# One low-part split in four by an accumulating DMA instead of VectorE, in the feed-forward weights of a hybrid decoder block

## The chip, the cores and the metric

The kernel runs on one core of a Trainium2 chip. Time is device time in microseconds (us) for one execution of the whole program. The engines are named as in the profile: PE is TensorE (matrix multiply; PEld its weight loads), DVE is VectorE, ACT is ScalarE, POOL is GpSimd, SP is SyncE, which here only issues DMAs.

## The reference

One layer of a decoder block, 256 tokens, model width 2048, all float32: a normalised input goes through an input projection into two token mixers (a Mamba-2 scan and a causal pooling), their outputs through an output projection; then a feed-forward part of width 5632, a residual add and a final norm. What matters here is the feed-forward part:

```python
def swiglu(h, w_gate, w_up, w_down):
    return (jax.nn.silu(h @ w_gate) * (h @ w_up)) @ w_down
...
h = h + swiglu(rms_norm(h, ffn_norm_w[i]), w_gate[i], w_up[i], w_down[i])
return rms_norm(h, final_norm_w)
```

The three weights are 2048 x 5632, 2048 x 5632 and 5632 x 2048 numbers; they are read from HBM once.

## The kernel before

The feature dimension lies on partitions, tokens on the free dimension. Every weight is multiplied as two float32r parts, `w = hi + lo`, and so is every activation; three of the four products are formed (`mm_part`, L191): for each k-tile of 128 rows and each block of 128 columns one matmul of `hi` with the activation's high and low parts side by side (512 columns, L206) and one of `lo` with the high part (256 columns, L214).

`WeightStream` (L37) makes those parts. Weights come in pieces, lists that are written out in the order of use (L127 to L168): for the feed-forward part 22 groups of 256 columns, each with two pieces of 8 k-tiles from `w_gate` and two from `w_up`, then 8 groups of `w_down` with five pieces of 8 k-tiles and one of 4. SP loads each piece into a raw buffer (three buffers, L67 and L74), and each piece is split in chunks of 4 k-tiles (128 x 1024 elements): ACT copies the raw chunk into `hi`, which rounds it (L89), and DVE subtracts, `lo = raw - hi` (L90). So there are 8 chunks in a gate and up pair, 4 each, and 11 in a down group: 264 in the feed-forward part.

`hi` and `lo` have three buffers each (`AHEAD`, L41). `next` (L95) hands chunk n to the matmuls and first emits the splits up to chunk n + 2; the split of a chunk can start when the matmuls of the chunk three before it have released its buffers. The engines work through their queues in order; a scheduler places the instructions, and the splits are marked to go early:

```python
with self.tc.high_priority():
    nc.scalar.copy(out=hi[:, :nk, :], in_=raw)
    nc.vector.tensor_tensor(
        out=lo[:, :nk, :], in0=raw, in1=hi[:, :nk, :].bitcast(F32), op=ALU.subtract)
```

After a gate or up group (`for f in range(NFG)`, L628) ACT and DVE take the sums out of PSUM: for gate a copy (L635), an add (L636), a multiplication (L637) and the SiLU on ACT (L638); for up a copy (L642), three DVE operations (L643 to L645), and the split of the hidden values into `hid` (L650, L651). Down groups end in `evac_add` (L599) and a few operations for the norm. POOL does almost nothing: four loads of the decays `E` (L488), the load of the residual `h` (L581), and one operation at the end.

Of the kernel before, what the change touches and what calls it, by code (L numbers as in the profile page):

```python
# [14 lines left out]
T = 256  # L15
# [11 lines left out]

# columns of the packed per-channel vectors
V_ATTN, V_CONVW, V_CONVB, V_DSKIP, V_SSDN, V_PSC, V_FFN, V_FIN, V_ALL = (
    0, 16, 112, 136, 152, 168, 184, 200, 216)  # L30

# 256-column groups of the input projection in the order they are consumed:
# B (0, 1), C (2, 3), u (4..11), then per SSD group two of x and two of z
G_U, G_XZ = 4, 12


class WeightStream:  # L37
    """Weights in order of use: loaded ahead, then split exactly into two
    float32r parts (w = hi + lo) in chunks of up to four k-tiles."""

    AHEAD = 3  # L41

    def __init__(self, tc, pool, pieces):
        self.tc, self.nc, self.pool = tc, tc.nc, pool
        # a piece is a list of (source, k-tiles) that are loaded into one buffer
        self.pieces = pieces
        self.chunks = []
        for p, srcs in enumerate(pieces):
            base = 0
            for i, (_, nk) in enumerate(srcs):  # L50
                k0 = 0
                while k0 < nk:
                    n = 2 if p == 0 and i == 0 else 4
                    self.chunks.append((p, base + k0, n))
                    k0 += n
                base += nk
        self.after_load = {}
        self.raw = {}
        self.split = {}
        self.loaded = 0  # L60
        self.done = 0
        self.pos = 0
# [17 lines left out]
    def split_to(self, n):  # L80
        nc = self.nc
        while self.done < min(n, len(self.chunks)):
            p, k0, nk = self.chunks[self.done]
            self.load_to(p + 3)
            raw = self.raw[p][:, k0:k0 + nk, :]
            hi = self.pool.tile([P, 4, 256], F32R, tag="hi", name=f"hi{self.done}", bufs=self.AHEAD)
            lo = self.pool.tile([P, 4, 256], F32R, tag="lo", name=f"lo{self.done}", bufs=self.AHEAD)
            with self.tc.high_priority():
                nc.scalar.copy(out=hi[:, :nk, :], in_=raw)  # L89
                nc.vector.tensor_tensor(  # L90
                    out=lo[:, :nk, :], in0=raw, in1=hi[:, :nk, :].bitcast(F32), op=ALU.subtract)
            self.split[self.done] = (hi, lo, nk)
            self.done += 1
# [9 lines left out]
def kernel(  # L103
# [22 lines left out]

# [1 line left out]
    pieces = []  # L128
# [29 lines left out]
    for g in range(2, 8):  # L158
        add_out(g, 1)
        add_out(g, 0)  # L160
    for f in range(NFG):
        for w in (w_gate, w_up):
            pieces.append([(w[f, :, 0:8, :], 8)])
            pieces.append([(w[f, :, 8:16, :], 8)])
    for g in range(8):
        for k in range(0, KF, 8):
            nk = min(8, KF - k)
            pieces.append([(w_down[g, :, k:k + nk, :], nk)])  # L168
    stream = WeightStream(tc, wpool, pieces)

# [1 line left out]
    vec_sb = const.tile([P, V_ALL], F32, name="vec_sb")  # L172
# [18 lines left out]
    def mm_part(ps, rhs, first, last, wide=True):  # L191
        """ps[b][:, 0:256] += w_hi x_hi + w_lo x_hi for the two 128-column blocks b, over
        the k-tiles whose [hi | lo] are in rhs; w_hi x_lo goes to ps[b][:, 256:512]
        when wide, and to ps[b][:, 0:256] too when not."""
        if not isinstance(ps, list):
            ps = [ps[:, 0, :], ps[:, 1, :]]
        k = 0
        n = len(rhs)
        while k < n:
            hi, lo, nk = stream.next()  # L200
            for b in range(2):
                cs = slice(b * P, (b + 1) * P)
                for j in range(nk):
                    st = first and k + j == 0
                    if wide:
                        nc.tensor.matmul(  # L206
                            ps[b], hi[:, j, cs], rhs[k + j],
                            start=st, stop=False, skip_group_check=True)
                    else:
                        for o in (0, T):  # L210
                            nc.tensor.matmul(  # L211
                                ps[b][:, 0:T], hi[:, j, cs], rhs[k + j][:, o:o + T],
                                start=(st and o == 0), stop=False, skip_group_check=True)
                    nc.tensor.matmul(  # L214
                        ps[b][:, 0:T], lo[:, j, cs], rhs[k + j][:, 0:T],
                        start=False, stop=(last and k + j == n - 1), skip_group_check=True)
            k += nk
# [6 lines left out]
    def rstd_stats(sqs, n, name):  # L224
        """1/sqrt(EPS + sum over partitions and over the list of sqs / n), with tokens on
        partitions, as the diagonals of two [128, 128] matrices."""
        pss = [pms.tile([P, 512], F32, tag="ms", name=f"ps{c}_{name}") for c in range(2)]
# [19 lines left out]
    def rstd_spread(stats, c=0):  # L247
        """The result of rstd_stats, [128, 256], the same on every partition, in PSUM."""
        pss, dg = stats
        ps = pss[c][:, T:512]  # L250
        nc.tensor.matmul(ps, ones, dg.rearrange("p c t -> p (c t)"), start=True, stop=True,
                         skip_group_check=True)
        return ps

    # ================= phase 1: norm, input projection, mixers =================
    xhl = big.tile([P, KD, 512], F32R, tag="big", name="xhl")
# [51 lines left out]
    def evac_in(ps, dst):  # L308
        """dst = ps * rstd for the two blocks of an input-projection group."""
        nc.vector.tensor_tensor(out=dst, in0=ps[:, :, 0:T], in1=bc_mid(r1, 2), op=ALU.mult)  # L310

    def conv_silu(dst, src, ct, pool):
        """dst = silu(causal depthwise conv of src) for channel tile ct."""
        o = pool.tile([P, T], F32, tag="cv", name="cv", bufs=2)
        w = [col(V_CONVW, 4 * ct + k) for k in range(4)]
        nc.scalar.activation(o, src, AF.Identity, scale=w[3], bias=col(V_CONVB, ct))
        for s in (1, 2, 3):
            tap = nc.vector.scalar_tensor_tensor(
                out=o[:, s:T], in0=src[:, 0:T - s], scalar=w[3 - s], in1=o[:, s:T],
                op0=ALU.mult, op1=ALU.add)  # L320
        return tap, nc.scalar.activation(dst, o, AF.Silu)
# [17 lines left out]

# [1 line left out]
    dtT = p1.tile([P, 2, NHEAD], F32, name="dtT")  # L341
    nacT = p1.tile([P, 2, NHEAD], F32, name="nacT")
    acum_d = dram.tile([NHEAD, T], F32, name="acum_d")
    with tc.tile_pool(name="pd", bufs=1) as pd:
# [20 lines left out]
        nc.vector.tensor_scalar(v, v, hvec_sb[:, 0:1], None, op0=ALU.add)  # L365
        # softplus(v) = max(v, 0) + log1p(e), e = exp(-|v|); log1p(e) = 2 atanh(e / (2 + e))
        nc.vector.scalar_tensor_tensor(out=e, in0=v, scalar=-1.0, in1=v, op0=ALU.mult, op1=ALU.max)
# [31 lines left out]
    def cb_group(g):  # L399
        """C B^T of a group: s in the first tile against all l, then s and l in the second."""  # L400
        cbp = pms.tile([P, 512], F32, tag="ms", name="cbp")
# [5 lines left out]
    def x_group(g, c):  # L407
        """A 256-column group of x, normalised; the conv comes later."""
        ps = mm_group(xk, f"x{g}_{c}", wide=False)
        xin = p1.tile([P, 2, T], F32, tag="xin", name="xin", bufs=2)  # L410
        evac_in(ps, xin)
        return xin

# [1 line left out]
    with tc.tile_pool(name="pp", bufs=1) as pp:  # L415
# [60 lines left out]

# [1 line left out]
    with tc.tile_pool(name="psd", bufs=1) as pssd:  # L478
# [5 lines left out]
        for g in range(NGRP):  # L484
            # log-decays, causal mask, exp
            E = pssd.tile([P, HPG, 384], F32, tag="E", name="E", bufs=1)
# [90 lines left out]

    # ================= phase 2: output projection, FFN, final norm =================
    p2 = ctx.enter_context(tc.tile_pool(name="p2", bufs=1))
# [10 lines left out]
    def add_sq(k):  # L590
        """ssq += squares of h1's k-tiles k, k + 1."""
        t2 = squares(k)
# [6 lines left out]
    def evac_add(ps, k):  # L599
        """h1[k, k + 1] += a + b."""  # L600
        tb = p2.tile([P, 2, T], F32, tag="tb2", name="tb2", bufs=2)
# [50 lines left out]

    # the last SiLU is done: bring in the square root's table before the tail needs it
    nc.scalar.activation(warm, hid[2][:, KF - 2 * KD - 1, T - 1:T].bitcast(F32), AF.Sqrt, scale=0.0)
# [81 lines left out]
```

## Time and profile before

| what | us |
|---|---|
| three executions | 1308.55, 1309.37, 1324.73 |
| their median | 1309.37 |
| span of the profiled execution | 1322.4 |
| PE busy in it | 1309.8 (99%) |
| DVE, ACT, POOL busy | 836.0 (63%), 665.6 (50%), 9.0 (1%) |

The profile is of one execution, whose span runs from its first instruction to its last. Only the execution of 1324.73 us is long enough to hold it, so that is taken as the profiled execution's own time: 2.3 us lie around the span. Busy times add up an engine's instructions; matmuls overlap, so a matmul's duration (0.40 us for 512 columns) is longer than the step from one to the next. A row names an instruction by its line, engine, operation, and output<-inputs. In square brackets stands how long the engine was idle before it and what ended that.

### The profile page before, as it was taken

Reading aid. Unit: us, or ns where it says so; the run is one execution under the profiler, and the core shown is the slowest. Engines: PE = TensorE matmul, PEld = TensorE weight load, DVE = VectorE, ACT = ScalarE, POOL = GpSimd, SP = SyncE. Lnnn points to the kernel's source line nnn. Section 1 sums busy time; section 2 is a strip of 40 time slices with the busy share of each in tenths; the row PEclk is TensorE's granted clock in tenths of the full one; section 3 lists DMA queues with packets and bytes.
Section 4 is the critical chain, followed back from the end, with each engine's and each line's share of the span. In section 5 each row is a group of like instructions: output and inputs, shape, how many; then the busy total and the mean of one; then the engine's idle time right before and its main releaser. Section 6 shows DMA issues by size and latency. Waiting matters only on the chain.

```text
span 1322.4 us, 20341 instructions
## 1 busy us (share of the span) xinstructions
PE 1309.8 (99%) x8490; PEld 1184.9 (90%) x8490; DVE 836.0 (63%) x1017; ACT 665.6 (50%) x823; POOL 9.0 (1%) x23
## 2 busy tenths in 40 slices
PE   9999999999999999999999999999999999999996
PEld 8999999999998888888888888888888888888896
DVE  6977877878776556565656556565656554555453
ACT  7644447677674444454444444444444444444442
POOL 0000000000000000000000000000000000000000
PEclk9999999999999999999999999999999999999998
DMA  8445556555546555555555555555555555555552
GB/s 301 157 164 188 191 178 212 186 193 186 196 160 250 181 180 187 189 186 187 177 188 186 191 192 188 180 182 186 187 191 191 186 181 181 199 176 184 198 176 80
DMA packets 36844, 247.08 MB, mean 187 GB/s; under 512 B 4080, under 2 KB 4368, under 8 KB 8976
## 3 DMA queue, kind: packets, MB, share of 16 engines
q1 hardware_dynamic: 35376, 239.10, 53.0%
q0 software_dynamic: 1232, 6.29, 1.3%
q8 instruction: 66, 1.08, 0.3%
q10 hardware_dynamic: 144, 0.39, 0.1%
q14 instruction: 26, 0.21, 0.0%
HBM read 243.64 MB, written 2.13 MB: 186 GB/s over the span
## 4 chain that ended last, share of the span: by engine, by line
PE 98%; DMA 1%; DVE 0%; SPq 0%; ACT 0%; issue 0%; DVEq 0%
PE up L206 13%; PE g L206 13%; PE d L206 11%; PE o L206 9%; PE d L214 6%; PE g L214 6%; PE up L214 6%; PE x L211 5%; PE u L211 5%; PE z L211 5%; PE o L214 5%; PE u L214 2%; PE x L214 2%; PE z L214 2%; PE bc L211 2%; PE d L211 2%
## 5 line engine op out<-in xcount | busy, mean ns | idle before, releaser
L90 DVE TENSOR_TENSOR lo<-raw,hi 128x1024 fp32r<-128x1024 f32 (+1 forms) x449 | 548.2, 1221 | 434.1 <-ACT hi L89 432.8
L89 ACT CAST hi<-raw 128x1024 fp32r<-128x1024 f32 (+1 forms) x449 | 469.9, 1047 | 597.2 <-PE d L206 122.1
L206 PE MATMUL g<-h1hl,hi 128*128 128x512 f32 x704 | 249.9, 399 | 0.0
L206 PE MATMUL up<-h1hl,hi 128*128 128x512 f32 x704 | 249.6, 399 | 0.0
L206 PE MATMUL d<-hid,hi 128*128 128x512 f32 x616 | 217.7, 399 | 0.0
L214 PE MATMUL d<-hid,lo 128*128 128x256 f32 x704 | 197.9, 281 | 0.0
L214 PE MATMUL g<-h1hl,lo 128*128 128x256 f32 x704 | 197.7, 281 | 0.0
L214 PE MATMUL up<-h1hl,lo 128*128 128x256 f32 x704 | 197.6, 281 | 0.0
L206 PEld LDWEIGHTS g<-h1hl,hi 128*128 128x128 f32 x704 | 132.3, 188 | 33.1
L206 PEld LDWEIGHTS up<-h1hl,hi 128*128 128x128 f32 x704 | 132.3, 188 | 32.9
L206 PEld LDWEIGHTS d<-hid,hi 128*128 128x128 f32 x616 | 115.7, 188 | 28.8
L214 PEld LDWEIGHTS g<-h1hl,lo 128*128 128x128 f32 x704 | 133.0, 189 | 0.0
L214 PEld LDWEIGHTS d<-hid,lo 128*128 128x128 f32 x704 | 133.0, 189 | 0.0
L214 PEld LDWEIGHTS up<-h1hl,lo 128*128 128x128 f32 x704 | 133.0, 189 | 0.0
L211 PE MATMUL z<-xhl,hi 128*128 128x256 f32 x512 | 93.3, 285 | 0.0
L211 PE MATMUL x<-xhl,hi 128*128 128x256 f32 x512 | 93.0, 284 | 0.0
L211 PE MATMUL u<-xhl,hi 128*128 128x256 f32 x512 | 93.0, 283 | 0.0
L206 PE MATMUL o<-yssd,hi 128*128 128x512 f32 x256 | 91.0, 399 | 0.0
L206 PE MATMUL o<-ypool,hi 128*128 128x512 f32 x256 | 90.6, 398 | 0.0
L211 PEld LDWEIGHTS x<-xhl,hi 128*128 128x128 f32 x512 | 79.8, 192 | 0.5 <-issue 0.5
L211 PEld LDWEIGHTS z<-xhl,hi 128*128 128x128 f32 x512 | 79.9, 192 | 0.2
L211 PEld LDWEIGHTS u<-xhl,hi 128*128 128x128 f32 x512 | 80.0, 192 | 0.0
(189 smaller groups left out, 1603.9 us busy)
## 6 DMA issues: line engine op xcount, KB each, us to landing
raw<-in_w_in_dram SPq DMA_DIRECT2D x52, 1024.0 KB, 5.0
raw<-in_w_gate_dram SPq DMA_DIRECT2D x44, 1024.0 KB, 5.0
raw<-in_w_up_dram SPq DMA_DIRECT2D x44, 1024.0 KB, 5.1
raw<-in_w_down_dram SPq DMA_DIRECT2D x40, 1024.0 KB, 4.8
raw<-in_w_out_dram SPq DMA_DIRECT2D x32, 1024.0 KB, 4.8
raw<-in_pool_w_dram SPq DMA_DIRECT2D x4, 1024.0 KB, 4.9
E<-acum_d POOLq DMA_DIRECT2D x4, 1024.0 KB, 5.9
raw<-in_w_down_dram SPq DMA_DIRECT2D x8, 512.0 KB, 3.3
```

The lines of the kernel that those rows point to most:

```text
L89: nc.scalar.copy(out=hi[:, :nk, :], in_=raw)
L90: nc.vector.tensor_tensor(out=lo[:, :nk, :], in0=raw, in1=hi[:, :nk, :].bitcast(F32), op=ALU.subtract)
L206: nc.tensor.matmul(ps[b], hi[:, j, cs], rhs[k + j], start=st, stop=False, skip_group_check=True)
L211: nc.tensor.matmul(ps[b][:, 0:T], hi[:, j, cs], rhs[k + j][:, o:o + T], start=(st and o == 0), stop=False, skip_group_check=True)
L214: nc.tensor.matmul(ps[b][:, 0:T], lo[:, j, cs], rhs[k + j][:, 0:T], start=False, stop=(last and k + j == n - 1), skip_group_check=True)
```

## The change

In chunks of four k-tiles that belong to a feed-forward piece and whose number is divisible by 4, `lo` is no longer made by DVE. ACT first writes `-hi` into `lo`; then POOL issues a DMA that reads the same weights from HBM a second time and adds them onto `lo`, so that `lo = -hi + w`. The raw piece is loaded as before, since `hi` is still made from it. The rest of the difference between the two files is comments that went, so that later lines move by 9.

```diff
+        self.dma_from = len(pieces)
...
             with self.tc.high_priority():
                 nc.scalar.copy(out=hi[:, :nk, :], in_=raw)
-                nc.vector.tensor_tensor(
-                    out=lo[:, :nk, :], in0=raw, in1=hi[:, :nk, :].bitcast(F32), op=ALU.subtract)
+                if p >= self.dma_from and self.done % 4 == 0 and nk == 4:
+                    src, _ = self.pieces[p][0]
+                    nc.scalar.mul(lo[:, :nk, :], hi[:, :nk, :].bitcast(F32), -1.0)
+                    nc.gpsimd.dma_start(lo[:, :nk, :], src[:, k0:k0 + nk, :], accum_op=ALU.add)
+                else:
+                    nc.vector.tensor_tensor(
+                        out=lo[:, :nk, :], in0=raw, in1=hi[:, :nk, :].bitcast(F32), op=ALU.subtract)
...
+    first_ffn = len(pieces)
     for f in range(NFG):
...
     stream = WeightStream(tc, wpool, pieces)
+    stream.dma_from = first_ffn
```

The feed-forward part begins with chunk 185, so the chunks 188, 192, and so on are meant: in a gate or up group always the fourth and last, in the down groups different ones, 22 each of gate, up and down.

ACT's queue around one gate group, before. `hi284` is the cast of that gate group's last chunk, `hi288` that of the last chunk of the up group after it, `g12` and `up11` are the sums that ACT takes out in between, and `hid1` is the split of the hidden values.

```order
L642 COPY tu_8173<-up11_8088 128x512
L89 CAST hi284_8203<-raw141_8089 128x1024
L650 CAST hid1_5975<-tu_8173 128x2x256
L89 CAST hi285_8225<-raw142_8131 128x1024
L89 CAST hi286_8245<-raw142_8131 128x1024
L89 CAST hi287_8273<-raw143_8181 128x1024
L635 COPY tg_8265<-g12_8180 128x512
L89 CAST hi288_8293<-raw143_8181 128x1024
L638 ACTIVATE tg_8265<-tg_8265 128x512
```

The same place after:

```order
L651 COPY tu_8197<-up11_8111 128x512
L91 CAST hi284_8227<-raw141_8112 128x1024
L94 ACTIVATE lo284_8228<-hi284_8227 128x1024
L659 CAST hid1_5975<-tu_8197 128x2x256
L91 CAST hi285_8250<-raw142_8155 128x1024
L91 CAST hi286_8270<-raw142_8155 128x1024
L91 CAST hi287_8298<-raw143_8205 128x1024
L644 COPY tg_8290<-g12_8204 128x512
L91 CAST hi288_8318<-raw143_8205 128x1024
L647 ACTIVATE tg_8290<-tg_8290 128x512
L94 ACTIVATE lo288_8319<-hi288_8318 128x1024
```

Two negations came in: in the gate chunk right behind its cast, in the up chunk behind its cast and the SiLU (`tg<-tg`). The order of the others is the same.

DVE's queue at the same place, before (`lo283` to `lo287` are subtractions of the chunks with these numbers):

```order
L90 TENSOR_TENSOR lo283_8184<-raw141_8089,hi283_8183 128x1024
L643 TENSOR_TENSOR tu_8173<-up11_8088,tu_8173 128x512
L644 TENSOR_TENSOR tu_8173<-tu_8173,r2_5973 128x512
L645 TENSOR_TENSOR tu_8173<-tu_8173,tg_8083 128x512
L90 TENSOR_TENSOR lo284_8204<-raw141_8089,hi284_8203 128x1024
L651 TENSOR_TENSOR hid1_5975<-tu_8173,hid1_5975 128x2x256
L90 TENSOR_TENSOR lo285_8226<-raw142_8131,hi285_8225 128x1024
```

And after, where `lo284` is gone from DVE:

```order
L97 TENSOR_TENSOR lo283_8208<-raw141_8112,hi283_8207 128x1024
L652 TENSOR_TENSOR tu_8197<-up11_8111,tu_8197 128x512
L653 TENSOR_TENSOR tu_8197<-tu_8197,r2_5973 128x512
L654 TENSOR_TENSOR tu_8197<-tu_8197,tg_8106 128x512
L660 TENSOR_TENSOR hid1_5975<-tu_8197,hid1_5975 128x2x256
L97 TENSOR_TENSOR lo285_8251<-raw142_8155,hi285_8250 128x1024
```

What stood around the subtraction `lo284` now follows on without it. The 66 accumulating DMAs stand one after another in POOL's queue, with nothing between them.

## Rows read from the trace of the kernel before

**Rows 1.** Busy us by engine, granted clock, DMA share and GB/s, feed-forward stretch.

```profile
core 0: us, PE busy (x) PEld busy (x) DVE busy (x) ACT busy (x) POOL busy (x), PEclk, DMA share, GB/s
568.00:1305.00 737.00, 737.00 (x4248) 642.85 (x4247) 418.48 (x431) 335.89 (x380) 0.00 (x0) 1.00 0.54 183
```

**Rows 2.** What PE waited for, whole span: us in total, times, longest us.

```profile
PE ps_r L251 <- DVE d_r L244: 1.8, 1, 1.8
...
PE bc L214 <- DVE lo L90: 1.0, 2, 0.8
...
```

**Rows 3.** Groups of instructions, 568 to 1305 us: the two halves of a split.

```profile
L90 DVE TENSOR_TENSOR lo<-raw,hi 128x1024 fp32r<-128x1024 f32 x260 | 318.4, 1225 | 312.3 <-ACT hi L89 312.1
L89 ACT CAST hi<-raw 128x1024 fp32r<-128x1024 f32 x260 | 273.0, 1050 | 387.0 <-PE d L206 122.1 <-PE g L206 117.1 <-PE up L206 107.6
```

**Rows 4.** Timeline of PE (start, duration, instruction): second and fourth chunk begun.

```profile
904.89 0.40 PE L206 MATMUL g<-h1hl,hi 128*128 128x512 f32 x1
...
910.78 0.28 PE L214 MATMUL g<-h1hl,lo 128*128 128x256 f32 x1
...
922.09 0.28 PE L214 MATMUL up<-h1hl,lo 128*128 128x256 f32 x1
```

**Rows 5.** Timeline of ACT, one gate and one up group.

```profile
904.97 1.05 ACT L89 CAST hi<-raw 128x1024 fp32r<-128x1024 f32 x1 [1.29 <-PE g L206]
...
916.28 1.05 ACT L89 CAST hi<-raw 128x1024 fp32r<-128x1024 f32 x1 [1.30 <-PE up L206]
917.24 0.63 ACT L638 ACTIVATE tg<-tg 128x512 f32<-128x512 f32 x1
919.15 1.05 ACT L89 CAST hi<-raw 128x1024 fp32r<-128x1024 f32 x1 [1.29 <-issue]
```

**Rows 6.** Timeline of DVE, the subtractions of the same chunks.

```profile
906.42 1.22 DVE L90 TENSOR_TENSOR lo<-raw,hi 128x1024 fp32r<-128x1024 f32 x1
...
917.36 1.23 DVE L90 TENSOR_TENSOR lo<-raw,hi 128x1024 fp32r<-128x1024 f32 x1 [0.28 <-ACT hi L89]
```

**Rows 7.** Issues of SP and POOL (timeline), and E's landing in two stretches.

```profile
201.15 0.33 SPq L74 DMA_DIRECT2D raw<-in_w_in_dram  x1
...
202.33 1.08 POOL L488 DMA_DIRECT2D E<-acum_d  x1 [0.30 <-issue]
...
E<-acum_d POOLq DMA_DIRECT2D x1, 1024.0 KB, 7.8
...
326.71 0.33 SPq L74 DMA_DIRECT2D raw<-in_w_in_dram  x1
...
330.32 0.88 POOL L488 DMA_DIRECT2D E<-acum_d  x1 [49.90 <-PE ps_y L542]
...
E<-acum_d POOLq DMA_DIRECT2D x1, 1024.0 KB, 5.4
...
907.67 0.33 SPq L74 DMA_DIRECT2D raw<-in_w_gate_dram  x1
```

**Rows 8.** DMA issues of the whole span: count, KB each, median us to landing.

```profile
raw<-in_w_gate_dram SPq DMA_DIRECT2D x44, 1024.0 KB, 5.0
...
E<-acum_d POOLq DMA_DIRECT2D x4, 1024.0 KB, 5.9
raw<-in_w_down_dram SPq DMA_DIRECT2D x8, 512.0 KB, 3.3
...
h<-in_x_dram POOLq DMA_DIRECT2D x1, 2048.0 KB, 9.4
```

**Rows 9.** Timeline in the down projection: a cast, and `lo` two chunks later.

```profile
1100.01 1.05 ACT L89 CAST hi<-raw 128x1024 fp32r<-128x1024 f32 x1 [1.77 <-PE d L206]
...
1105.82 0.28 PE L214 MATMUL d<-hid,lo 128*128 128x256 f32 x1
```

**Rows 10.** Busy us and granted clock (before the last two numbers), end of the span.

```profile
1311.00:1314.00 3.00, 1.21 (x8) 1.01 (x7) 1.51 (x9) 0.50 (x2) 0.00 (x0) 1.00 0.00 0
1315.00:1316.00 1.00, 0.00 (x0) 0.00 (x0) 1.00 (x2) 0.00 (x0) 1.00 (x1) 0.50 0.53 184
```

## The prediction

> **What bounds the kernel now.** I read the busy table by stretch first. In the feed-forward stretch, 568 to 1305 us, TensorE (PE) is busy 737.0 of 737.0 us at granted clock 1.00, VectorE (DVE) 418.5 and ScalarE (ACT) 335.9, and the DMA engines run at a share of 0.54 [rows 1]. Then I read who waited for whom, for PE alone over the whole span: it has five rows, 4.6 us in all, the longest of 1.8 us, and the longest that names a split is 1.0 us, for a low part of the first input group, at the very start [rows 2]. None lies in the feed-forward part. So the subtraction that the change takes away is on no path that sets the end: nothing can be gained there, and the question is only whether the new way delivers `lo` in time.
>
> The time it has comes from the timeline. 260 casts in 737.0 us [rows 3, 1] make a chunk of four k-tiles every 2.83 us. `hi` and `lo` have three buffers, so the split of chunk n starts when PE leaves chunk n-3: PE begins the second chunk of a gate group at 904.89, and ACT begins the cast for the group's fourth chunk at 904.97 [rows 4, 5]. PE's first `lo` matmul of that fourth chunk is at 910.78 [rows 4], 5.8 us later. Today the subtraction begins at 906.42 and takes 1.22 [rows 6], so `lo` is there at 907.64, 3.1 us early. Those 3.1 us are all the cover there is.
>
> **The change part by part.** The condition picks 66 of the 264 feed-forward chunks (22 x 8 of gate and up, 8 x 11 of down): the last chunk of each of 22 gate and 22 up groups, and 22 in the down projection.
>
> *Removed:* 66 subtractions of 1225 ns [rows 3], 81 us of DVE. DVE stands idle there and PE never waits for it in this stretch [rows 1, 2], so it is worth 0.
>
> *Added on ACT:* 66 negations, 128x1024 from SBUF to SBUF. I price one as the cast of that size, 1050 ns [rows 3]: 69 us on an engine with 401 of 737 us free [rows 1]. By itself 0. But it stands in front of the DMA, and ahead of it in an up group stands the SiLU, which the order puts between cast and negation.
>
> *Moved:* the raw buffer's second half is now last read by ACT's cast, not by DVE, so SP can issue the next load earlier: at about 906.1 instead of 907.67 [rows 7]. That load has time to spare: issued at 907.67 it would land 5.0 later [rows 8], and the first cast that reads it is the one at 919.15 [rows 5]. But it now begins 1 us ahead of the accumulating DMA, on the same 16 engines.
>
> *Added wait:* the first `lo` matmul of such a chunk waits for the DMA instead of DVE, and all of PE queues behind it. On POOL only the next such DMA is queued, and on DVE nothing: the splits of the two chunks after it were released by chunks already passed.
>
> The time left between negation and need, with 0.03 us for each hand-over between engines (cast begun 916.28, 1.05 long, DVE off at 917.36 [rows 5, 6]):
> - gate: 904.97 + 1.05 + 0.03 + 1.05 + 0.03 = 907.13; needed at 910.78; **3.65 us left**.
> - up: cast at 916.28, but the SiLU ends at 917.24 + 0.63 = 917.87 [rows 5]; + 1.05 + 0.03 = 918.95; needed at 922.09 [rows 4]; **3.14 us left**.
> - down: 1100.01 + 2.16 = 1102.17; needed at 1105.82 [rows 9]; **3.65 us left**.
>
> Call L the time from POOL's issue to landing. Each late chunk stops PE by L minus what is left, and nothing gives it back: the next such split starts only when PE has passed the next chunk, so the stalls add up. Together: 22 x (L - 3.65) + 22 x (L - 3.14) + 22 x (L - 3.65), which is 66 L - 230 us once all are late.
>
> The trace has no accumulating DMA, so L is bounded. *Below:* a plain 512 KB load by SP lands in 3.3 us [rows 8]; only the up chunks would be late, 22 x 0.16 = 4 us. *Above:* POOL's 2 MB load lands in 9.4 us [rows 8]; 22 x (5.75 + 6.26 + 5.75) = 391 us. An end below nothing is excluded, since PE has no wait in the stretch that could go [rows 1, 2]. *Between:* an accumulate must fetch 512 KB from HBM and the 512 KB that it adds to, twice what a plain load fetches, so the nearest row is POOL's 1 MB transfer, median 5.9 us [rows 8]. Its four cases differ by what runs beside them: 5.4 when SP had issued a load 3.6 us before (326.71 against 330.32), 7.8 when one had been issued 1.2 us before (201.15 against 202.33) [rows 7]. In the gate and up groups the raw load goes out 1 us ahead, as in the second, though that was also POOL's first DMA; I take the middle, 6.6. In the down projection the chunk is as often the first of its buffer as the second, and I take the median, 5.9. Sum: 22 x 2.95 + 22 x 3.46 + 22 x 2.25 = **191 us**.
>
> One page supports the doubling, though no run here shows it: the Trainium skill, "Collectives: The Full Stack", section on the bandwidth ceiling, says that a reducing DMA is slower because it reads two sources, and reaches about half the rate of a copy.
>
> Only the slowest of the three runs, 1324.73 us, can hold a span of 1322.4; so 2.3 us lie around it, and it is 15.4 above the median of 1309.37. On its own scale the sum is 1324.7 + 191 = 1516. The stalls don't depend on where those 15 us lie, so for the median 1309.4 + 191 = 1500.
>
> **The rivals.**
>
> *Hidden: not slower.* The DMA lands within the 3.1 to 3.6 us that are left. For it: SP's 512 KB in 3.3 us [rows 8], the smallest transfer near this size. Against it: every transfer that POOL issued took 5.4 us or more [rows 7, 8], and an accumulate of 512 KB fetches as much as their smallest, 1 MB. Price: 0 to 4 us, 1309 to 1313. It decides below L = 3.9, where 66 L - 230 passes 26 us, 2% (about what a measurement of this kernel can tell from no change). A rule speaks for it, which stands by itself: the Trainium skill, "DMA: Bandwidth & Descriptors", section on the anatomy of one SWDGE DMA, gives a POOL-issued DMA 2.0 us plus its bytes at 436 GB/s, an estimate of 3.2 us for 512 KB; by that the sum is about 1 us. It would give E's 1 MB 4.4 us, and the trace has 5.4 to 7.8 [rows 7], so the trace disagrees with it even for a plain copy.
>
> *Much slower: the stalls lower PE's clock, or the accumulate runs at a quarter of a copy's rate.* After the last matmuls the granted clock reads 1.00 over three us in which PE worked 1.21, and 0.50, the 1.2 GHz level, from 1315 on, with PE idle [rows 10]. If each stall let it fall and the next chunk ran at half speed, 66 x 2.83 = 187 us come on top: 1687. A DMA with L of 9.4 gives 1700. Against the clock: stalls of 3 us would stand between runs of 11 us of unbroken work. The rule beside it: the Trainium skill, "TensorE: Matmul & The Clock Gate", part 1, says that the low level is the default and that activity lifts it; the last rows agree in that the clock falls once PE rests, and don't show whether a stall this short is enough.
>
> *Barely late.* L between 3.9 and 4.7, between SP's 512 KB and POOL's cleanest 1 MB: 27 to 80 us, 1336 to 1390. For it: half of E's bytes are written. Against it: the contention with the raw load.
>
> **How the numbers follow.** L between 4.7 and 9.1, time between 1390 and 1680: 0.76, with 1500 its middle by the rows. Hidden: 0.06. Barely late: 0.05. Much slower: 0.13. The range 1390 to 1680 leaves out 0.24 by these, of which part of the last (a fallen clock with a quick DMA) ends inside it, so about 0.2. Chances: slower by over 2% is the sum of the first, third and fourth, 0.94; within 2% 0.05; faster 0.01, since nothing waits for what was removed.
>
> **What would show it.** Right, if PE's waits have one new row, `lo` matmuls waiting for a DMA, 66 times and some 190 us, all in the feed-forward stretch; if `lo<-in_w_gate_dram` lands 6 to 7 us after issue and `lo<-in_w_down_dram` sooner than that; if the period of four chunks is 11.3 plus about 3 us; if the clock stays at 1.00; and if the first 568 us are as before. The SiLU step is right if up chunks wait about 0.5 us longer than gate chunks. Wrong, if that wait is missing (L under 3.6), if ACT or the raw loads, not the new DMA, end PE's waits, or if the clock column falls inside the stretch.

## The result and the profile after

The changed kernel takes 1594.7 us (median of 4 runs, 1588.44 to 1605.86) against 1310.42 before; the ratio on record is 1.208, 95% interval 1.201 to 1.214. It was forecast at 1500, between 1390 and 1680. The kernel before took 1309 to 1311 us in three of its four runs here, but 1324.73 in the profiled one and 1323 to 1327 beside the experiments below, so that the two medians divide to 1.217 and not to the ratio on record, and each experiment is told by its ratio to the runs beside it.

The stretches of the changed kernel (busy us of PE, PEld, DVE, ACT, POOL, then granted clock, DMA share, GB/s), to set against [rows 1]:

```profile
0.00:568.00 568.00, 565.28 (x4191) 535.15 (x4192) 410.37 (x571) 328.05 (x439) 7.76 (x23) 1.00 0.56 194
568.00:1575.00 1007.00, 810.63 (x4297) 695.91 (x4295) 344.24 (x370) 401.35 (x450) 56.33 (x66) 0.93 0.58 168
```

Up to 568 us nothing changed. All that was lost lies behind it, in two columns: PE stands idle for 196 of the 1007 us, and its clock reads 0.93 on the mean, not 1.00. What PE waited for (us in total, times, longest), to set against [rows 2]:

```profile
PE g L223 <- DMA lo<-in_w_gate_dram: 76.8, 22, 4.5
PE up L223 <- DMA lo<-in_w_up_dram: 60.0, 22, 3.9
PE d L223 <- DMA lo<-in_w_down_dram: 59.3, 22, 5.5
```

66 new waits, one for each DMA, 196.1 us together. PE's busy time went from 1309.8 to 1378.0, by 68.2, with the same 8490 matmuls. The two make 264.3, and the spans differ by 1586.4 - 1322.4 = 264.0: nothing else is lost. POOL's queue (packets, MB, share of 16 engines' span) and the landings (count, KB, median us), to set against [rows 8]:

```profile
q0 software_dynamic: 10736, 40.90, 13.2%
...
lo<-in_w_gate_dram POOLq DMA_DIRECT2D x22, 512.0 KB, 6.9
lo<-in_w_up_dram POOLq DMA_DIRECT2D x22, 512.0 KB, 5.9
lo<-in_w_down_dram POOLq DMA_DIRECT2D x22, 512.0 KB, 5.5
```

One up chunk and one gate chunk on the timelines of ACT, SP and POOL, to set against [rows 5]:

```profile
1015.43 1.05 ACT L91 CAST hi<-raw 128x1024 fp32r<-128x1024 f32 x1 [1.63 <-PE up L215]
1016.39 0.63 ACT L647 ACTIVATE tg<-tg 128x512 f32<-128x512 f32 x1
1016.92 1.04 ACT L94 ACTIVATE lo<-hi 128x1024 fp32r<-128x1024 f32 x1
...
1016.51 7.23 SPq L76 DMA_DIRECT2D raw<-in_w_up_dram  x2
...
1018.26 0.86 POOL L95 DMA_DIRECT2D lo<-in_w_up_dram  x1 [16.33 <-ACT lo L94]
...
1029.33 1.05 ACT L91 CAST hi<-raw 128x1024 fp32r<-128x1024 f32 x1 [0.89 <-PE g L215]
1030.41 1.06 ACT L94 ACTIVATE lo<-hi 128x1024 fp32r<-128x1024 f32 x1
...
1030.40 0.33 SPq L76 DMA_DIRECT2D raw<-in_w_gate_dram  x1
...
1031.77 0.86 POOL L95 DMA_DIRECT2D lo<-in_w_gate_dram  x1 [12.65 <-ACT lo L94]
```

From the start of the cast to POOL's issue it is 2.83 us in the up chunk and 2.44 in the gate chunk. By the kernel before, `lo` is needed 5.81 us after the cast begins [rows 4, 5], so 2.98 and 3.37 us are left, against the 3.14 and 3.65 of the prediction: the hand-over from ACT to POOL takes 0.30 us (1031.77 less the negation's end, 1031.47), ten times what was put down.

The stall behind one gate chunk and the next one, behind an up chunk, in the columns of the stretches above:

```profile
1004.50:1008.25 3.75, 0.00 (x0) 0.00 (x0) 1.23 (x1) 0.71 (x1) 0.00 (x0) 1.00 0.85 166
1008.50:1009.50 1.00, 1.00 (x7) 0.87 (x7) 0.00 (x0) 0.00 (x0) 0.00 (x0) 0.99 0.81 328
1009.50:1012.50 3.00, 3.00 (x11) 2.62 (x10) 0.00 (x0) 0.23 (x1) 0.00 (x0) 0.50 0.40 167
1013.00:1016.00 3.00, 3.00 (x19) 2.58 (x18) 2.52 (x3) 1.37 (x3) 0.00 (x0) 1.00 0.01 3
1021.75:1024.00 2.25, 0.01 (x1) 0.00 (x0) 1.23 (x1) 0.38 (x1) 0.00 (x0) 1.00 0.73 144
1024.50:1027.00 2.50, 2.50 (x15) 2.15 (x14) 0.00 (x0) 0.10 (x1) 0.00 (x0) 1.00 0.93 301
```

PE waits 3.8 us; its clock still reads 1.00 when it begins again, falls a microsecond later to 0.50 (1.2 of 2.4 GHz), and PE then has 11 matmuls in 3 us where it has 19 at full speed. After the shorter stall the clock stays at 1.00. I counted the falls from the start of each of the 66 stalls to 5 us after its end: of 10 stalls under 2 us none was followed by a fall, of 23 between 2 and 3 us five, of 33 longer ones 29. By the clock column 0.07 / 0.50 x 1007 = 141 us ran at the lower level, which costs half of it, 70, as an estimate; PE's busy time grew by 68.

### The profile page after: what moved, and what is told of

Its sections match the earlier page's. It is cut to its first block, busy times and chain, and to the rows that moved or that the text cites. A ratio compares the mean times of both kernels' runs of the same rounds, so it can differ in the third digit from the quotient of the medians.

```text
span 1586.4 us, 20485 instructions
## 1 busy us (share of the span) xinstructions
PE 1378.0 (87%) x8490; PEld 1232.2 (78%) x8490; DVE 759.7 (48%) x951; ACT 730.0 (46%) x889; POOL 65.9 (4%) x89
## 3 DMA queue, kind: packets, MB, share of 16 engines
q0 software_dynamic: 10736, 40.90, 13.2%
## 4 chain that ended last, share of the span: by engine, by line
PE 70%; DMA 26%; ACT 1%; issue 1%; DVE 0%; SPq 0%; DVEq 0%; ACTq 0%; POOLq 0%
DMA lo<-in_w_gate_dram 10%; DMA lo<-in_w_down_dram 8%; DMA lo<-in_w_up_dram 8%; PE o L215 8%; PE up L215 8%; PE g L215 7%; PE d L215 6%; PE g L223 4%; PE up L223 4%; PE d L223 4%; PE x L220 4%; PE u L220 4%; PE z L220 4%; PE o L223 4%; PE u L223 2%; PE x L223 2%
## 5 line engine op out<-in xcount | busy, mean ns | idle before, releaser
L97 DVE TENSOR_TENSOR lo<-raw,hi 128x1024 fp32r<-128x1024 f32 (+1 forms) x383 | 467.4, 1221 | 732.8 <-ACT hi L91 731.4
L223 PE MATMUL g<-h1hl,lo 128*128 128x256 f32 x704 | 213.3, 303 | 76.8 <-DMA lo<-in_w_gate_dram 76.8
L215 PE MATMUL g<-h1hl,hi 128*128 128x512 f32 x704 | 274.0, 425 | 0.0
L215 PE MATMUL up<-h1hl,hi 128*128 128x512 f32 x704 | 261.6, 412 | 0.0
L223 PE MATMUL d<-hid,lo 128*128 128x256 f32 x704 | 207.8, 295 | 59.3 <-DMA lo<-in_w_down_dram 59.3
L223 PE MATMUL up<-h1hl,lo 128*128 128x256 f32 x704 | 206.0, 293 | 60.0 <-DMA lo<-in_w_up_dram 60.0
L215 PE MATMUL d<-hid,hi 128*128 128x512 f32 x616 | 229.7, 413 | 0.0
L223 PEld LDWEIGHTS g<-h1hl,lo 128*128 128x128 f32 x704 | 147.0, 209 | 84.7 <-DMA lo<-in_w_gate_dram 83.7
L223 PEld LDWEIGHTS d<-hid,lo 128*128 128x128 f32 x704 | 141.5, 201 | 66.0 <-DMA lo<-in_w_down_dram 65.9
L215 PEld LDWEIGHTS g<-h1hl,hi 128*128 128x128 f32 x704 | 145.4, 207 | 32.9
```

The lines of the kernel that those rows point to most:

```text
L97: nc.vector.tensor_tensor(out=lo[:, :nk, :], in0=raw, in1=hi[:, :nk, :].bitcast(F32), op=ALU.subtract)
L215: nc.tensor.matmul(ps[b], hi[:, j, cs], rhs[k + j], start=st, stop=False, skip_group_check=True)
L223: nc.tensor.matmul(ps[b][:, 0:T], lo[:, j, cs], rhs[k + j][:, 0:T], start=False, stop=(last and k + j == n - 1), skip_group_check=True)
```

## The experiments

Theory: PE loses what the DMA lands late, chunk by chunk, and the clock falls because of those stalls. Rivals: the traffic, the extra ACT work or the chip's load is the cost.

**Four buffers.** To make room, three small tiles of the feed-forward part (`t2`, `tb2`, `tu`) have one buffer in place of two.

```diff
-    AHEAD = 3
+    AHEAD = 4
...
```

> Four buffers for hi and lo in place of three, so a split can start one chunk (2.83 us) earlier. Theory (PE loses what the accumulating DMA lands late, nothing else): 6.5 us are left in gate and down, 6.0 in up, against landings of 6.9, 5.9 and 5.5 us; PE's waits for the DMA fall from 196 us to under 25, the clock stays at 1.00, and the time is 1315 to 1340. Rival (the extra traffic or the extra ACT work is itself the cost): the waits move to hi or to the raw loads, and the time stays above 1400.

Ratio 1.028 (1.026 to 1.030), PE's waits:

```profile
PE g L223 <- DMA lo<-in_w_gate_dram: 9.5, 12, 1.9
PE d L223 <- DMA lo<-in_w_down_dram: 8.1, 8, 2.7
PE up L223 <- DMA lo<-in_w_up_dram: 4.7, 12, 1.7
```

The same DMAs move the same bytes, and one chunk more of lead takes the waits from 196 to 22.3 us and the time from 20.8% above the kernel before to 2.8%. The loss of 36 us is a little over the 6 to 31 that 1315 to 1340 stood above 1309.4.

**Four buffers and the hi matmuls first.** In the 66 chunks the loop runs over the blocks twice, once for `hi` and once for `lo`:

```diff
...
-            for b in range(2):
+            late = (stream.pos - 1) in stream.by_dma
+            for b, part in ((0, "hi"), (1, "hi"), (0, "lo"), (1, "lo")) if late else ((0, "both"), (1, "both")):
...
```

> Four buffers, and in the chunks with the DMA the eight hi matmuls ahead of the eight lo matmuls, which puts the first lo matmul another 1.5 us back. Theory: 8.0 us are left, more than the longest landing seen (7.9); PE's waits for the DMA are under 5 us and the time is that of the kernel before, 1308 to 1318. Rival (the traffic or ACT is the cost): above 1400. A gain below the kernel before is expected by neither, PE having been busy throughout.

Ratio 1.0028 (1.0017 to 1.0039); clock 0.997, as before. PE's waits for the DMA are down to this:

```profile
PE g L228 <- DMA lo<-in_w_gate_dram: 0.6, 3, 0.2
PE d L228 <- DMA lo<-in_w_down_dram: 0.5, 1, 0.5
```

So 66 DMAs more, 65 us more busy time on ACT and 75 us less on DVE change the time by 0.3% once `lo` comes in time. It isn't faster than the kernel before, as PE was never free there. The gate DMAs even land later here (7.6 us at the median), at no cost.

**The turned order alone, three buffers.**

> The changed kernel with three buffers, and only the order turned in its 66 chunks: eight hi matmuls, then eight lo. Theory: 1.5 us more are left each time, waits 196 - 66 x 1.5 = about 100 us, and with shorter stalls the clock falls rarely; time 1405 to 1440. Rival (the DMA lands later by what PE gives it, since the raw loads move with PE): waits above 150 us, time above 1500.

Ratio 1.086 (1.083 to 1.090), 1440.8 us, waits 32.7 + 32.5 + 23.5 = 88.7 us: the waits are a little under the 100 that were expected, and the time is 0.8 us over the upper end.

**No addition.** The same DMA without `accum_op`, so that `lo` holds `w` and not `w - hi` in these chunks.

```diff
-  nc.gpsimd.dma_start(lo[:, :nk, :], src[:, k0:k0 + nk, :], accum_op=ALU.add)
+  nc.gpsimd.dma_start(lo[:, :nk, :], src[:, k0:k0 + nk, :])
```

> The same DMA without its addition: lo receives w and not w - hi, so the subtraction is left out in these chunks; ACT's negation stays. Theory (adding costs a second fetch, as the prediction had it): landings shorter by about 1.5 us, PE's waits 196 to about 100 us, fewer falls of the clock, time 1400 to 1460. Rival (the landing is POOL's issue, the way and the raw load beside it, and the addition is free): landings within 0.3 us of 6.9, 5.9 and 5.5, time 1575 to 1605.

Ratio 1.095 (1.093 to 1.098), 1450.0 us, waits 94.6 us, as the theory had it. The landings and the DMA time of POOL's queue (share of 16 engines' span):

```profile
q0 software_dynamic: 10736, 40.90, 8.5%
...
lo<-in_w_gate_dram POOLq DMA_DIRECT2D x22, 512.0 KB, 5.2
lo<-in_w_up_dram POOLq DMA_DIRECT2D x22, 512.0 KB, 5.0
lo<-in_w_down_dram POOLq DMA_DIRECT2D x22, 512.0 KB, 4.2
```

The addition costs 0.9 to 1.7 us of landing. With it the same packets took 13.2% of 1586.4 us, without it 8.5% of 1448.1; less the 17 us that E and h took in the kernel before (1.3% of 1322.4), that is 2.9 us of all engines for one accumulating DMA and 1.6 for a plain one. The Trainium skill's rule that a reducing DMA runs at about half a copy's rate ("Collectives: The Full Stack", the bandwidth ceiling) agrees with that. The Trainium skill's formula for a POOL-issued DMA ("DMA: Bandwidth & Descriptors", the anatomy of one SWDGE DMA), by which 512 KB take an estimated 3.2 us, doesn't: even the plain one needs 4.2 or more beside the raw loads.

**Spare matmuls into the stall.**

```diff
...
             hi, lo, nk = stream.next()
+            if (stream.pos - 1) in stream.by_dma:
+                spare = pms.tile([P, 512], F32, tag="ms", name="spare")
+                for i in range(10):
+                    nc.tensor.matmul(spare, hi[:, i % nk, 0:P], rhs[k], start=True, stop=True, skip_group_check=True)
```

> Ten spare matmuls of 512 columns (about 2.1 us, into a PSUM tile that nobody reads) in PE's queue ahead of each chunk with the DMA. Theory (the clock falls because PE stands idle in the stall): the clock reads 1.00, PE's waits for the DMA drop to about 60 us since the spare work fills the rest, and the time is 1505 to 1545, some 70 below the changed kernel, with more work. Rival (the clock follows the DMA traffic or the load on the chip, not the idle time): clock 0.95 as before, time 1580 to 1610.

Ratio 1.180 (1.176 to 1.185), 1561.9 us. One set, and the feed-forward stretch:

```profile
1010.60 2.44 PE L215 MATMUL spare<-h1hl,hi 128*128 128x512 f32 x10
...
1012.88 0.39 PE L221 MATMUL up<-h1hl,hi 128*128 128x512 f32 x1
1015.02 0.39 PE L229 MATMUL up<-h1hl,lo 128*128 128x256 f32 x1 [1.76 <-DMA lo<-in_w_up_dram]
...
568.00:1540.00 972.00, 901.68 (x4879) 764.41 (x4878) 343.50 (x366) 399.71 (x446) 55.68 (x65) 0.99 0.60 174
```

With 660 matmuls more and the same DMAs the clock reads 0.99 in place of 0.93 and the ratio falls from 1.208 to 1.180. So it is PE's idleness that lowers the clock, not the traffic. The gain is smaller than expected: a set holds PE for 2.28 us (1010.60 to 1012.88), 150 in all, and 70.1 us of waits remain, 220 where the stalls were 196.

**Late without a DMA.** DVE makes `lo` in the 66 chunks, by the same subtraction several times over; no negation, no DMA.

```diff
-                    nc.scalar.mul(lo[:, :nk, :], hi[:, :nk, :].bitcast(F32), -1.0)
-                    nc.gpsimd.dma_start(lo[:, :nk, :], src[:, k0:k0 + nk, :], accum_op=ALU.add)
+                    for _ in range(6):
+                        nc.vector.tensor_tensor(
+                            out=lo[:, :nk, :], in0=raw, in1=hi[:, :nk, :].bitcast(F32), op=ALU.subtract)
```

> No DMA and no negation: in the same 66 chunks DVE makes lo by the same subtraction six times over (five of them extra, 6.1 us). Worked out from the timeline of the kernel before, lo is late by 3.0 us in gate and 2.6 in up and down: PE's waits 180 us, now for DVE. Theory (a stall of this length lets the clock fall, whatever made it): some 15 to 35 falls, clock about 0.95 to 0.97, time 1525 to 1570. Rival (the falls belong to the DMA traffic): clock 1.00, time 1485 to 1500.

> As the one before with five subtractions: lo late by 1.8 us in gate, 1.4 in up and down, 100 us in all. Theory (in the changed kernel none of the ten stalls under 2 us was followed by a fall): clock 1.00, time 1400 to 1420. Rival (any stall lowers it in some cases): clock under 0.98, time above 1430.

Ratios 1.145 (1.144 to 1.147) and 1.090 (1.088 to 1.092). The times missed, 1517.9 us against 1525 or more for the six-fold one: the scheduler spread the extra subtractions between DVE's other work, so that the stalls are small in gate and up and long in down. That tells the two causes apart all the same (six times over, gate and up, then a part of down):

```profile
568.00:1000.00 432.00, 404.66 (x2234) 340.88 (x2233) 419.50 (x424) 183.15 (x209) 0.00 (x0) 1.00 0.50 167
1300.00:1480.00 180.00, 135.12 (x715) 117.41 (x713) 118.39 (x110) 52.03 (x58) 0.00 (x0) 0.88 0.35 120
...
PE d L223 <- DVE lo L94: 99.4, 19, 8.3
...
PE up L223 <- DVE lo L94: 11.0, 20, 0.8
PE g L223 <- DVE lo L94: 8.9, 20, 0.5
```

Without one accumulating DMA the clock falls to 0.88 in the part with long stalls: all 18 stalls of 4 us and more were followed by a fall, none of the 45 shorter waits for `lo`. The five-fold one took 1443.9 us at a clock of 0.97, the figures of its rival, but it doesn't test what it was meant to: it has 15 stalls of 3 to 4 us, 11 of them with a fall, where stalls under 2 us were planned.

**Raw loads left out.** `raw` of later feed-forward pieces is an earlier piece's buffer, without a load: in the first run for all after the first three pieces, in the other two for every second one of gate and up.

> In the feed-forward part only the first three raw pieces are loaded, and all later pieces split those same buffers again: 133 raw loads are left out, all else stays. Theory (the raw load on the same 16 DMA engines lengthens the landing): landings fall to about 5.2 us in gate, up and down alike, PE's waits from 196 to 100 to 125 us, time 1410 to 1460. Rival (no contention, gate is later for another reason): landings stay at 6.9, 5.9 and 5.5, time 1575 to 1605.

> In the gate and up part every second raw load is left out (the split reads the piece before it again), so that each remaining load is released by the chunk two after the one with the DMA: a load comes only behind the accumulating DMA's start, none ahead of it. Down is as in the changed kernel. Theory A (the gate chunk lands late because the raw load issued 1.4 us ahead holds the engines): gate's landing falls from 6.9 to about 5.7, as without any raw loads. Theory B (the load that starts while the DMA runs is what delays its end): gate stays at 6.4 to 7.0.

> The other half of the loads left out: each remaining load is released by the cast of the chunk with the DMA itself and goes out about 1.4 us ahead of it, and none comes behind. Theory A (the load ahead): gate's landing stays at 6.4 to 7.0 and up's at about 6. Theory B (the load behind): gate's landing falls to about 5.7, as without any raw loads.

The first took 1518.4 us, a ratio of 1.142 (1.136 to 1.148), with 145.2 us of waits in the profiled execution of 1502.67 us; the other two 1559.7 and 1623.3, one execution each. Waits and landings of the first, then the landings with loads only behind, then with loads only ahead:

```profile
PE up L227 <- DMA lo<-in_w_up_dram: 50.4, 22, 2.6
PE g L227 <- DMA lo<-in_w_gate_dram: 47.7, 22, 2.5
PE d L227 <- DMA lo<-in_w_down_dram: 47.1, 22, 2.7
...
lo<-in_w_gate_dram POOLq DMA_DIRECT2D x22, 512.0 KB, 5.6
lo<-in_w_up_dram POOLq DMA_DIRECT2D x22, 512.0 KB, 5.7
lo<-in_w_down_dram POOLq DMA_DIRECT2D x22, 512.0 KB, 5.5
```

```profile
lo<-in_w_gate_dram POOLq DMA_DIRECT2D x22, 512.0 KB, 5.7
lo<-in_w_up_dram POOLq DMA_DIRECT2D x22, 512.0 KB, 5.7
```

```profile
1018.37 0.33 SPq L80 DMA_DIRECT2D raw<-in_w_up_dram  x1
...
1019.73 0.86 POOL L99 DMA_DIRECT2D lo<-in_w_gate_dram  x1 [14.65 <-ACT lo L98]
...
lo<-in_w_gate_dram POOLq DMA_DIRECT2D x22, 512.0 KB, 7.1
lo<-in_w_up_dram POOLq DMA_DIRECT2D x22, 512.0 KB, 6.3
```

With no raw loads beside it the DMA lands in 5.5 to 5.7 us wherever it stands, more than the 5.2 that I expected and so with longer waits than the 125 and a time above the range. The load that goes out 1.4 us ahead is what makes it 7 in gate: theory A. (A load behind goes out only 5.4 us after the DMA, at 1007.45 against 1002.02 in the run with loads only behind, when the DMA has all but landed.) It is the change itself that put this load there, since the raw buffer's release no longer waits for DVE.

## Why the prediction was right, and where it was not

*Bound, and what is removed.* Right: what DVE was spared, 81 us of subtractions, bought nothing, and PE's only new waits are for the DMA, 66 times. (The 1.0 us that the prediction calls the longest wait for a split is the total of two; the longest is 0.8 [rows 2]. Nothing rests on it.)

*The sum of the stalls.* 191 us forecast, 196 measured, but by errors that cancel, so that a hit this close is luck. A gate chunk waited 76.8 / 22 = 3.49 us where 2.95 stood, an up chunk 2.73 where 3.46 stood, a down chunk 2.70 where 2.25 stood: 12 us more, 16 less and 10 more in all. The hand-over between engines was put at 0.03 us, from ACT to DVE; from ACT to POOL it is 0.30, which takes 0.28 us from what was left in a gate chunk and 0.16 in an up chunk. And L was 6.9, 5.9 and 5.5 where 6.6, 6.6 and 5.9 stood. These are medians: in down the longest wait is 5.5 us, so that chunks wait longer on the mean than the median landing gives. Taking 512 KB with an addition for a 1 MB transfer was sound: 5.6 us without company against E's 5.4.

*The SiLU.* Wrong in its sign: up chunks were to wait 0.5 us longer than gate chunks and waited 0.8 less (60.0 against 76.8 us, 22 each). The SiLU does put the DMA off, by 0.39 us, but two things outweigh that. First, the DMA starts 1.75 and not 1.37 us behind the raw load, and lands in 5.9 instead of 6.9 (6.3 instead of 7.1 in the run with loads only ahead; 5.7 and 5.6 without raw loads). Second, the prediction took PE's order for unchanged. In 19 of the 22 up chunks the scheduler put two matmuls of the next gate group ahead of the late one. In the kernel before, the first `lo` matmul of such a chunk at 922.09 [rows 4] comes straight behind a `hi` matmul:

```profile
921.85 0.40 PE L206 MATMUL up<-h1hl,hi 128*128 128x512 f32 x1
```

In the changed kernel:

```profile
1021.00 0.40 PE L215 MATMUL up<-h1hl,hi 128*128 128x512 f32 x1
1021.24 0.40 PE L215 MATMUL g<-h1hl,hi 128*128 128x512 f32 x1
1021.48 0.28 PE L223 MATMUL g<-h1hl,lo 128*128 128x256 f32 x1
1024.08 0.39 PE L223 MATMUL up<-h1hl,lo 128*128 128x256 f32 x1 [2.33 <-DMA lo<-in_w_up_dram]
```

`lo` was due at 1015.43 + 5.81 = 1021.24, and there PE has a pair of other matmuls, about 0.35 us of work (2.83 / 8), before it stalls. That nearly makes up for the SiLU: without raw loads, up and gate chunks wait almost alike, 50.4 and 47.7 us in all.

*The clock.* The step that failed is "the clock stays at 1.00". That was the reason why 1500 was the middle and not 1570, and the fall had been put among the rivals, at 187 us if every stall brought one. 34 of 66 did, for 68 us, 2.0 each where 2.83 stood. A clock column that falls inside the stretch is one of the prediction's own signs of being wrong. "Against the clock: stalls of 3 us would stand between runs of 11 us of unbroken work" was no protection: with such runs before them, 29 of 33 stalls over 3 us were followed by a fall. The Trainium skill's rule that the low level is the default and activity lifts it ("TensorE: Matmul & The Clock Gate", part 1) is what the spare matmuls bear out, with 0.99 in place of 0.93.

*The base.* 1500 stands on 1309.4. On the profiled execution's own scale the prediction has 1516; with 68 of clock and 5 of stalls that makes 1589, and 1588.44 was measured. So these two terms are all that the sum lacked on that scale; why the median of the kernel before lies 15 us under its profiled execution, no run here shows.

*Hidden.* It didn't come about, and the run with four buffers and the turned order shows what was enough: one chunk, 2.83 us, and the eight `hi` matmuls that come first, put at 1.5 us, together 4.3 us more of lead.

## What to carry to other kernels

A step off the critical path can be moved to a slower way only if the lead covers that way's latency: count from the release of the buffer to the first use, with every hand-over and with what else is on the DMA engines, before counting the work it saves. On an engine that is busy throughout, a stall costs more than its length when the clock falls behind it; shortening the stalls (from 196 to 89 us by order alone) gave back most of both: the mean clock of the span rose from 0.952 to 0.986. Where the freed engine was no bound, even the perfectly hidden form gains nothing.

## What the runs showed of the hardware

- PE's clock may still read 1.00 through a stall and fall only after PE has started again (24 of the 34 falls of the changed kernel, up to 1.5 us later), and it doesn't fall with every stall. The length of the stall orders it without a sharp edge: with raw loads only behind, 24 of 49 stalls of 2.0 to 2.5 us were followed by a fall, with no raw loads 11 of 54. What decides between them stays open.
- Ten matmuls with no use ahead of each late chunk took the mean clock of the feed-forward stretch from 0.93 to 0.99 and the ratio to the kernel before from 1.208 to 1.180.
- An accumulating 512 KB DMA from HBM onto SBUF lands in 5.6 us with no raw loads beside it and in 7.1 us when a 1 MB load was issued 1.4 us before it; a plain one beside the same loads is 0.9 to 1.7 us faster.
- From the end of ACT's negation to POOL's issue of the DMA that waits for it, 0.30 us pass.
